# Whole gathered rows of V for the second 128 tokens, and one pass over V for the first 128

## Chip, cores and metric

The kernel runs on 1 core of one Trainium2 chip. The metric is the device time of one execution in microseconds (us); the profile is one execution taken by the hardware profiler.

## The reference, cut to what matters

The program is two transformer blocks over 256 tokens of width 1024, in float32. Only the last layer of the second block, a product-key expert layer, is touched by the change:

```python
def block(xb):                       # xb: 128 tokens x 1024; called for 2 blocks of tokens
    ...                              # query, top 16 of 2 x 128 keys, top 16 of 16 x 16, in 8 heads
    idx = ...                        # 128 tokens x 8 heads x 16 experts, out of 16384 experts
    gate = jax.nn.softmax(best_s, axis=-1)
    h = jax.nn.gelu(jnp.einsum('thkd,td->thk', u_table[idx], xb), approximate=False)
    return jnp.einsum('thk,thkd->td', gate * h, v_table[idx])
```

u_table and v_table are 16384 rows of 1024 floats each (64 MB per table). Each token picks 128 rows (slots) of both. The layer's result is added to x (times ALPHA) and a layer norm ends the kernel.

## The kernel before, in words

**Tokens and slots.** Tokens stand on the 128 partitions, in two blocks t = 0 and t = 1. `gather(dst, tab, idx, s)` (line 1377) is an indirect DMA from POOL's queue that fetches, for slot s, one table row for each of the 128 tokens: 512 KB for whole rows, 256 KB for half rows.

**U.** For each slot, `u_dot` (line 1404) gathers a row of U for each token and lets DVE multiply it with x and sum it (line 1408). For some slots `u_mm` (line 1380) has PE transpose the gathered rows (1392), ACT copy them (1393) and PE multiply them with x (1396); `u_diag` (1399) has DVE pick the diagonal. `weights` (1420) turns the sums into coefficients by a Gelu on ACT and a product on DVE.

**V as a dense product.** `AT[t]` is a matrix of coefficients, 128 tokens x 16384 experts, made from one-hot rows by `spread_low` (ACT, 1425) and `spread` (DVE, PE, ACT, 1432), 32 groups each for a token block. With it, a sum over chosen rows becomes a product with all of V: 128 blocks of 128 rows, in PE matmuls with 512 columns, two instructions for each.

**The order of the last stages.** DVE's order is that of the program text (`manual_schedule`); the other engines' order is fixed when the kernel is built. Gathers stand one behind the other on POOL's queue, and loads of V on SP's.

1. The loop of lines 1509 to 1525 handles U for t = 0.
2. The loop of lines 1592 to 1627 handles U for t = 1, slot n by slot n: 18 slots with n below 36 by `u_mm`, 110 by `u_dot`. In steps 0 to 35 it also spreads AT[0] (32 groups, LOW = 36); in steps 0 to 63 (SEL = 64) it advances the selection (`later`) of the last three pairs of heads of t = 1 by 47 items in 18 steps and 94 items in 46 steps; from step 38 `hdense` multiplies AT[0] with the upper 512 columns of V (line 1581), whose 64 loads of 512 KB (two row blocks of half rows each, line 1569) go through 4 to 6 buffers. At n = 64 two constants of the last norm are loaded on POOL's queue (line 94), into memory that the selection used. The gathered rows of U have 6 buffers in pool `ub`, and 8 more in pool `sec` up to step 64.
3. Lines 1643 to 1674: the coefficients of t = 1, then the second half of the making of AT[1] (`high1`).
4. Lines 1719 to 1737: the lower 512 columns of V are loaded (line 1636, 64 loads of 512 KB) and multiplied with AT[0] and AT[1] (line 1641). The upper 512 columns for t = 1 are fetched as gathered half rows (`v_load`, 128 gathers of 256 KB) and added by DVE (`v_add`, line 1466). The layer norm of t = 0 (`end`) runs beside the last steps, that of t = 1 at the end.

Of the kernel before, what the change touches and what calls it, by code (L numbers as in the profile page):

```python
# [23 lines left out]
def block_kernel(ctx: ExitStack, tc: tile.TileContext, I, out):  # L24
    nc = tc.nc
# [1117 lines left out]
    vhalf = vtab.rearrange("e (a d) -> (e a) d", a=2)  # L1143
    io = pe_.tile([128, 128], F, name="io")
    G.iota(io, pattern=[[1, 128]], base=0, channel_multiplier=0, allow_small_or_imprecise_dtypes=True)
    idx_u, idx_v, ex_all, gate_all, hd_all, sc_all, c_all, tr_all = ({} for _ in range(8))
    for t in range(2):
        idx_u[t] = pe_.tile([128, 128], I32, name=f"idxu{t}")
        idx_v[t] = pe_.tile([128, 128], I32, name=f"idxv{t}")
# [178 lines left out]
    def select(t, h0, nh, early=False):  # L1328
# [33 lines left out]
        V.tensor_scalar(idx_v[t][:, hs], idx_u[t][:, hs], 2.0, 1.0, op0=OP.mult, op1=OP.add)  # L1362
# [5 lines left out]
    def u_tile(t, s):  # L1368

        if t and second and s % 7 >= 3:  # L1370
            return second[0].tile([128, D], F, tag="u", name="ust", bufs=8)
        if t == 0 and s % 3 == 2:
            return ux.tile([128, D], F, tag="u", name="ust")
        return ub.tile([128, D], R, tag="u", name="u").bitcast(F)
# [5 lines left out]
    def u_mm(t, s):  # L1380
# [51 lines left out]
    def spread(t, q):  # L1432
# [4 lines left out]
        both = q % (3 if t == 0 else 2) == 0  # L1437
# [99 lines left out]

    secx = ExitStack()
    sec = secx.enter_context(tc.tile_pool(name="sec", bufs=1, side="right"))
    xF1 = sec.tile([128, 8, 128], F, name="xF1")  # L1540
    for c in range(2):
        A.activation(out=xF1[:, 4 * c:4 * c + 4], in_=half_T(x2[:, 1], c), func=AF.Copy)
    second += [sec, xF1]
# [12 lines left out]
    hs_, hb = {}, iter(range(64))  # L1556

    def hload():
        b = next(hb, None)
        if b is None:  # L1560
            return
        if late_h:
            w = ub.tile([128, D], R, tag="u", name="wh").bitcast(F)
        elif second and b % 6 >= 4:
            w = sec.tile([128, D], F, tag="h", name="wh", bufs=2)
        else:
            w = h_tile("wh")
        hs_[b] = w.rearrange("p (b c) -> p b c", b=2)
        nc.sync.dma_start(out=hs_[b], in_=vtab[b * 256:(b + 1) * 256, 512:].rearrange("(b p) c -> p b c", p=128))

    hn = iter(range(64))

    def hdense():
        b = next(hn, None)
        if b is None:
            return False
        hload()
        w = hs_.pop(b)
        for i in range(2):
            n = b * 2 + i  # L1580
            T.matmul(acc2, lhsT=AT[0][:, :, n], rhs=w[:, i], start=n == 0, stop=n == 127)  # L1581
        return True

    late_h = []
    s2 = chain(*(select(1, h, 2) for h in (2, 4, 6)))
    SEL, LOW, HN = 64, 36, 38

    H1 = 58
    MMS1 = range(1, LOW, 2)

    later = chain(paced(s2, TWO, 18), paced(s2, 2 * TWO, SEL - 18))
    for n in range(128):
        assert (1, n // 16) in ready
        if n in MMS1:
            due[n + 5] = (u_mm(1, n), 1, n)
        else:
# [9 lines left out]
        if n == LOW - 10:  # L1606
            for _ in range(6):
                hload()
        if n >= HN:
            m, k = 128 - HN, n - HN  # L1610
            for _ in range(k * H1 // m, (k + 1) * H1 // m):
                hdense()
        if n == SEL:
# [15 lines left out]
    late_h.append(1)
    acc = [pa(), pa()]  # L1630
    wt = {}

    def vload(b):
        w = ub.tile([128, D], R, tag="u", name="w").bitcast(F)
        wt[b] = w.rearrange("p (b c) -> p b c", b=2)
        nc.sync.dma_start(out=wt[b], in_=vtab[b * 256:(b + 1) * 256, 0:512].rearrange("(b p) c -> p b c", p=128))

    def dense(t, b):
        for i in range(2):
            n = b * 2 + i  # L1640
            T.matmul(acc[t], lhsT=AT[t][:, :, n], rhs=wt[b][:, i], start=n == 0, stop=n == 127)  # L1641

    weights(1, 0, 128)
# [5 lines left out]
    left = [128]

    def v_next():
        s = next(vq, None)
        if s is not None:
            ahead.append((s, v_load(s)))
        if not ahead:
            return False
        s, v = ahead.pop(0)
        v_add(s, v)
        left[0] -= 1
        if not left[0]:  # L1660
            V.bn_stats(out=st[:, 1, 1], in_=x2[:, 1, 512:])
        return True

    PRE = 6
    for q in high1:
        spread(1, q)
        if q % 2 == 0:
            hdense()
        if q >= 4:
            v_next()  # L1670
    while hdense():
        v_next()
    for b in range(PRE):
        vload(b)
    V.scalar_tensor_tensor(x2[:, 0, 512:], x2[:, 0, 512:], ALPHA, acc2, op0=OP.mult, op1=OP.add)
    V.bn_stats(out=st[:, 0, 1], in_=x2[:, 0, 512:])
    o2 = out[0].rearrange("(t p) d -> t p d", p=128)

    def low_half(t):
        z = x2[:, t, :512]  # L1680
        if t == 0:
            V.scalar_tensor_tensor(z, z, ALPHA, acc[t], op0=OP.mult, op1=OP.add)
        else:
            V.tensor_tensor(z, z, acc[t], op=OP.add)
        yield
        V.bn_stats(out=st[:, t, 0], in_=z)
# [83 lines left out]
```

## Time and profile before

| | |
|---|---|
| median of 3 runs | 1452.6 us (1452.05 to 1454.0) |
| the profiled execution | 1450.03 us, of which the span of its instructions is 1448.3 us |
| busy share of the span | PE 89%, PE weight loads 73%, DVE 67%, ACT 41%, POOL 31% |
| bytes moved by DMA | 338.58 MB, 234 GB/s over the span |
| mean granted TensorE clock | 0.975 of full speed |

The shares are means over stages with different limits, so the last 560 us have to be read by stages. Of the two DMA queues that matter, q0 carries what POOL issues (gathers) and q1 what SP issues (loads of weights and of V).

### The profile page before, as it was taken

The numbers are of one execution on the slowest core, as the hardware profiler recorded it, in microseconds if no ns is written. First come the engines' busy times: TensorE is split into PE (matmuls) and PEld (weight loads), VectorE is DVE, ScalarE is ACT, GpSimd is POOL, SyncE is SP. The second block draws the span as 40 slices with busy tenths as digits, with TensorE's granted clock in tenths as the row PEclk, the third lists the DMA queues.
The fourth block names the chain that finished last, engine by engine and source line by source line (L and its number), as shares of the span: only waits on it lengthen the run. The fifth ranks groups of instructions, "written<-read, shape, count | busy, mean of one in ns | idle before, by whom it ended". The sixth has DMA issues, their size and how long they took to land.

```text
span 1448.3 us, 20024 instructions
## 1 busy us (share of the span) xinstructions
PE 1290.2 (89%) x7068; PEld 1056.9 (73%) x7068; DVE 974.5 (67%) x2345; ACT 590.0 (41%) x1194; POOL 451.0 (31%) x420
## 2 busy tenths in 40 slices
PE   8999999998999999998998955997765697999996
PEld 7988998976897778987888855894432366666664
DVE  5687655577575486587899987989766549555303
ACT  6465544464455731232232398770292036000000
POOL 2000000001000000003678876544454236777301
PEclk9999999999999999998999977999999999999999
DMA  7435555555454330065999999879999976999741
GB/s 235 146 117 181 188 189 186 188 166 161 141 160 136 113 101 1 7 196 203 361 346 370 330 364 349 271 234 357 404 407 408 375 258 170 368 331 348 259 158 69
DMA packets 132821, 338.58 MB, mean 234 GB/s; under 512 B 11675, under 2 KB 15089, under 8 KB 132721
## 3 DMA queue, kind: packets, MB, share of 16 engines
q1 hardware_dynamic: 83680, 165.01, 34.7%
q0 software_dynamic: 48288, 170.98, 32.3%
q10 hardware_dynamic: 752, 1.31, 0.3%
q8 instruction: 56, 0.92, 0.3%
q14 instruction: 45, 0.36, 0.1%
HBM read 336.21 MB, written 1.05 MB: 233 GB/s over the span
## 4 chain that ended last, share of the span: by engine, by line
PE 69%; DMA 13%; ACT 9%; DVE 7%; issue 1%; SPq 0%; DVEq 0%; ACTq 0%
PE pa L1641 15%; DMA wh<-in_peer_v_dram 10%; PE pa L217 8%; PE pa L219 8%; PE pa L218 8%; PE pa L1396 4%; PE pb L1448 3%; PE pa L1581 3%; ACT AT L1429 3%; PE pb L217 2%; PE pb L219 2%; PE pb L218 2%; PE pa L1187 2%; PE pb L963 2%; DMA AT<-in_peer_w_q_dram 2%; ACT uT L1393 1%
## 5 line engine op out<-in xcount | busy, mean ns | idle before, releaser
L212 DVE TENSOR_TENSOR w<-raw,w 128x1024 fp32r<-128x1024 f32 (+2 forms) x162 | 197.7, 1224 | 117.9 <-ACT w L211 117.4
L211 ACT ACTIVATE w<-raw 128x1024 fp32r<-128x1024 f32 (+2 forms) x164 | 172.9, 1061 | 168.8 <-PE pa L219 68.9
L1377 POOL DMA_INDIRECT u<-in_peer_u_dram,idxu x178 | 198.2, 1113 | 126.6 <-DVE jk L1408 60.0
L1408 DVE SCALAR_TENSOR_TENSOR jk<-u,xa 128x1024 bf16<-128x1024 f32 x159 | 193.7, 1218 | 51.3 <-DMA u<-in_peer_u_dram,idxu 50.7
L1641 PE MATMUL pa<-w,AT 128*128 128x512 f32 x512 | 222.7, 595 | 1.0 <-ACT AT L1449 0.7
L1641 PEld LDWEIGHTS pa<-w,AT 128*128 128x128 f32 x512 | 150.4, 296 | 68.8 <-DMA w<-in_peer_v_dram 2.1
L1581 PE MATMUL pa<-wh,AT 128*128 128x512 f32 x256 | 128.5, 639 | 63.1 <-DMA wh<-in_peer_v_dram 62.4
L1377 POOL DMA_INDIRECT v<-in_peer_v_dram,idxv x128 | 134.6, 1052 | 78.1 <-issue 25.4
L1581 PEld LDWEIGHTS pa<-wh,AT 128*128 128x128 f32 x256 | 72.3, 298 | 118.5 <-DMA wh<-in_peer_v_dram 94.7
L1396 PE MATMUL pa<-xF,uT 128*128 128x128 f32 x800 | 112.6, 298 | 28.3 <-ACT uT L1393 26.7
L1466 DVE SCALAR_TENSOR_TENSOR xa<-v,c,xa 128x512 f32<-128x512 f32 x128 | 96.0, 750 | 59.6 <-DMA v<-in_peer_v_dram,idxv 58.0
L1396 PEld LDWEIGHTS pa<-xF,uT 128*128 128x128 f32 x800 | 102.6, 207 | 38.7 <-ACT uT L1393 38.3
L1377 POOL DMA_INDIRECT ust<-in_peer_u_dram,idxu x78 | 94.8, 1215 | 61.6 <-PE pb L1392 29.3
L94 POOL DMA_DIRECT2D ln_g<-in_ln_g_dram x2 | 1.1, 572 | 291.0 <-PE pb L1105 285.0
L1702 ACT ACTIVATE xa<-xa,nmu 128x512 f32<-128x512 f32 x3 | 2.1, 716 | 206.6 <-DVE nmu L1696 206.6
L1429 ACT ACTIVATE AT<-io,tr 128x128 f32<-128x128 f32 x256 | 82.4, 402 | 0.4 <-DVE jk L1408 0.3
L1448 PE MATMUL pb<-e,AT 128*128 128x128 f32 x512 | 68.9, 280 | 11.6 <-ACT e L1447 11.5
L217 PE MATMUL pb<-xt,w 128*128 128x256 f32 (+2 forms) x272 | 77.0, 283 | 0.0
L218 PE MATMUL pb<-xt,w 128*128 128x256 f32 (+2 forms) x272 | 76.7, 282 | 0.0
L219 PE MATMUL pb<-xt,w 128*128 128x256 f32 (+2 forms) x272 | 76.6, 281 | 0.0
L1448 PEld LDWEIGHTS pb<-e,AT 128*128 128x128 f32 x512 | 63.0, 191 | 17.2 <-ACT e L1447 14.1
L217 PE MATMUL pa<-w,xt 128*128 128x512 f32 x176 | 71.6, 412 | 1.4 <-ACT w L211 1.0
(534 smaller groups left out, 2752.8 us busy)
## 6 DMA issues: line engine op xcount, KB each, us to landing
raw<-in_mlp_w_dram SPq DMA_DIRECT2D x64, 512.0 KB, 3.6
wh<-in_peer_v_dram SPq DMA_DIRECT2D x64, 512.0 KB, 12.7
w<-in_peer_v_dram SPq DMA_DIRECT2D x64, 512.0 KB, 6.7
raw<-in_w_in_dram SPq DMA_DIRECT2D x38, 512.0 KB, 3.5
raw<-in_mlstm_w_in_dram SPq DMA_DIRECT2D x20, 512.0 KB, 3.6
AT<-in_peer_w_q_dram SPq DMA_DIRECT2D x12, 512.0 KB, 19.1
raw<-in_mlstm_w_out_dram SPq DMA_DIRECT2D x8, 512.0 KB, 3.8
raw<-in_ple_gate_w_dram SPq DMA_DIRECT2D x8, 512.0 KB, 3.8
```

What stands on the lines that cost most here:

```text
L211: A.activation(out=w1[:, :kn * cn], in_=raw[:, :kn * cn], func=AF.Copy)
L212: (eng or V).tensor_tensor(w2[:, :kn * cn], raw[:, :kn * cn], w1[:, :kn * cn].bitcast(F), op=OP.subtract)
L217: T.matmul(o, lhsT=a1, rhs=b1, start=start, stop=False)
L218: T.matmul(o, lhsT=a1, rhs=b2, start=False, stop=False)
L219: T.matmul(o, lhsT=a2, rhs=b1, start=False, stop=stop)
L1377: G.indirect_dma_start(out=dst, out_offset=None, in_=tab, in_offset=bass.IndirectOffsetOnAxis(ap=idx[:, s:s + 1], axis=0))
L1396: T.matmul(o[:, :128], lhsT=uT[:, k], rhs=xT[:, k], start=k == 0, stop=k == 7)
L1408: V.scalar_tensor_tensor(jk, u, 1.0, x2[:, t], op0=OP.mult, op1=OP.mult, accum_out=hd_all[t][:, s:s + 1])
L1429: A.activation(out=g[:, n], in_=io, func=AF.Square, bias=tr_all[t][:, 1, q * 4 + n:q * 4 + n + 1])
L1448: T.matmul(ps[:, i * 128:(i + 1) * 128], lhsT=g[:, i], rhs=e1[:, i], start=True, stop=True)
L1581: T.matmul(acc2, lhsT=AT[0][:, :, n], rhs=w[:, i], start=n == 0, stop=n == 127)
L1641: T.matmul(acc[t], lhsT=AT[t][:, :, n], rhs=wt[b][:, i], start=n == 0, stop=n == 127)
```

## The change

For t = 1, V is no longer multiplied with a coefficient matrix: all 1024 columns of each chosen row are gathered (128 gathers of 512 KB) and added by DVE. AT[1], its making, the second index table `idx_v` and the product of t = 1 with the lower half of V go. For t = 0, V is loaded once in whole rows (128 loads of 512 KB) and each block is multiplied in two halves, into two PSUM tiles. The gathered rows of t = 1, first of U and then of V, share one ring of 13 buffers (`ring1`); the loads of V use the 6 buffers of `ub` and the 4 of `wraw`, 9 loads ahead. All 128 slots of t = 1 go by `u_dot`. AT[0] is spread in 24 steps instead of 36. `blocks_at` spreads the 128 blocks evenly over steps 24 to 243 of the two loops (128 slots of U, then 128 of V).

```diff
-        if t and second and s % 7 >= 3:
-            return second[0].tile([128, D], F, tag="u", name="ust", bufs=8)
+        if t:
+            return ring1[0].tile([128, D], F, tag="u", name="u1", bufs=13)
...
     def v_load(s):
-        if not vts:
-            w = h_tile("v")
-            vts[1], v = w[:, 512:], w[:, :512]
-        else:
-            v = vts.pop(1)
-        gather(v, vhalf, idx_v[1], s)
+        v = u_tile(1, s)
+        gather(v, vtab, idx_u[1], s)
         return v
...
-        z = x2[:, 1, 512:]
-        V.scalar_tensor_tensor(z, v, c_, z, op0=OP.mult, op1=OP.add)
+        z = x2[:, 1]
+        V.scalar_tensor_tensor(z, v, c_all[1][:, s:s + 1], z, op0=OP.mult, op1=OP.add)
...
+    ring1.append(ctx.enter_context(tc.tile_pool(name="ring1", bufs=1, side="right")))
...
+    def vload():
+        n = next(to_load, None)
+        if n is not None:
+            held[n] = h_tile("w") if n % 5 in (1, 3) else ub.tile([128, D], R, tag="u", name="w").bitcast(F)
+            nc.sync.dma_start(out=held[n], in_=vtab[n * 128:(n + 1) * 128, :])
+
+    def dense():
...
+        vload()
+        w = held.pop(n)
+        for c in range(2):
+            T.matmul(acc[c], lhsT=AT[0][:, :, n], rhs=w[:, c * 512:c * 512 + 512], start=n == 0, stop=n == 127)
...
-    SEL, LOW, HN = 64, 36, 38
+    SEL, LOW, AHEAD = 64, 24, 9
...
+    LAST = 244
+
+    def blocks_at(n):
+        for _ in range((n - LOW) * 128 // (LAST - LOW), (n + 1 - LOW) * 128 // (LAST - LOW)):
+            dense()
+
     for n in range(128):
         assert (1, n // 16) in ready
-        if n in MMS1:
-            due[n + 5] = (u_mm(1, n), 1, n)
-        else:
-            u_dot(1, n)
-        if n in due:
-            u_diag(*due.pop(n))
+        u_dot(1, n)
...
+        if n == 8:
+            for _ in range(AHEAD):
+                vload()
+        if n >= LOW:
+            blocks_at(n)
         if n == SEL:
...
-            at1 = ctx.enter_context(tc.tile_pool(name="at1", bufs=1, side="right"))
-            AT.append(at1.tile([128, 128, 128], F, name="AT1"))
-            for i in range(2):
-                slots_T(1, ex_all[1][:, i], i)
...
+        if n == 100:
+            weights(1, 0, 64)
...
     A.activation(out=x2[:, 1], in_=x2[:, 1], func=AF.Copy, scale=ALPHA)
...
+    END = 118
+    end = chain(half_sum(0), half_sum(1), last_norm(0))
+    ahead = [v_load(s) for s in range(12)]
+    for s in range(128):
+        if s < 116:
+            ahead.append(v_load(s + 12))
+        v_add(s, ahead.pop(0))
+        if s == 8:
+            weights(1, 64, 128)
+        blocks_at(128 + s)
+        if s >= END:
+            advance(end)
```

## Rows read from the trace of the kernel before

**Rows 1.** Page, part 4: the chain that ended last, by engine and line.
```profile
PE 69%; DMA 13%; ACT 9%; DVE 7%; issue 1%; SPq 0%; DVEq 0%; ACTq 0%
PE pa L1641 15%; DMA wh<-in_peer_v_dram 10%; PE pa L217 8%; PE pa L219 8%; PE pa L218 8%; PE pa L1396 4%; PE pb L1448 3%; PE pa L1581 3%; ACT AT L1429 3%; PE pb L217 2%; PE pb L219 2%; PE pb L218 2%; PE pa L1187 2%; PE pb L963 2%; DMA AT<-in_peer_w_q_dram 2%; ACT uT L1393 1%
```

**Rows 2.** The same chain in order of time: start us, us, engine and line.
```profile
991.63 17.41 DMA wh<-in_peer_v_dram
...
1166.95 10.68 DMA w<-in_peer_v_dram
...
1227.41 209.82 PE pa L1641 x488
```

**Rows 3.** Stretches: length; PE, PEld, DVE, ACT, POOL busy us (instructions); PE clock, DMA share, GB/s.
```profile
740.00:780.00 40.00, 37.19 (x311) 34.71 (x310) 38.11 (x128) 12.99 (x28) 32.27 (x26) 1.00 0.95 344
780.00:820.00 40.00, 35.27 (x283) 33.04 (x282) 37.61 (x120) 9.18 (x22) 32.46 (x25) 0.96 0.98 366
...
850.00:880.00 30.00, 15.94 (x89) 14.98 (x88) 26.25 (x56) 30.00 (x89) 23.14 (x21) 0.73 0.96 352
...
940.00:960.00 20.00, 19.21 (x165) 18.40 (x165) 16.66 (x60) 14.42 (x36) 9.78 (x10) 1.00 0.75 240
...
1000.00:1020.00 20.00, 12.22 (x26) 7.18 (x26) 19.96 (x55) 0.69 (x4) 8.31 (x7) 1.00 1.04 404
...
1120.00:1140.00 20.00, 10.45 (x20) 5.50 (x20) 12.46 (x21) 0.00 (x0) 9.82 (x11) 1.00 1.04 409
...
1230.00:1270.00 40.00, 40.00 (x94) 27.52 (x94) 22.18 (x31) 0.00 (x0) 31.08 (x30) 1.00 0.98 357
```

**Rows 4.** DMA queues from 1040 to 1100 us: packets, MB, share of 16 engines.
```profile
q0 software_dynamic: 4369, 15.93, 66.4%
q1 hardware_dynamic: 4366, 8.42, 36.9%
```

**Rows 5.** Timeline of DVE: slots 0, 36, 63 and 64 of t = 1.
```profile
892.10 1.22 DVE L1408 SCALAR_TENSOR_TENSOR jk<-u,xa 128x1024 bf16<-128x1024 f32 x1
...
975.98 1.22 DVE L1408 SCALAR_TENSOR_TENSOR jk<-u,xa 128x1024 bf16<-128x1024 f32 x1
...
1024.99 1.22 DVE L1408 SCALAR_TENSOR_TENSOR jk<-u,xa 128x1024 bf16<-128x1024 f32 x1
...
1026.25 1.22 DVE L1408 SCALAR_TENSOR_TENSOR jk<-u,xa 128x1024 bf16<-128x1024 f32 x1
```

**Rows 6.** Groups on DVE, 892 to 977 us: busy us, mean ns, idle before.
```profile
L1439 DVE TENSOR_TENSOR e<-tr,io 128x512 f32<-128x512 f32 x21 | 14.3, 679 | 5.4 <-PE pb L1448 5.4
L1445 DVE TENSOR_SCALAR e<-io,tr 128x128 f32<-128x128 f32 x44 | 12.2, 354 | 2.8 <-PE pb L1448 2.8
...
L1401 DVE SCALAR_TENSOR_TENSOR jk<-pa,ident 128x128 bf16<-128x128 f32 x15 | 4.4, 291 | 0.5
```

**Rows 7.** Timeline of POOL between the two U loops: start us, us, [idle before].
```profile
877.94 0.96 POOL L1377 DMA_INDIRECT u<-in_peer_u_dram,idxu  x1 [0.30 <-issue]
879.21 0.96 POOL L1377 DMA_INDIRECT u<-in_peer_u_dram,idxu  x1 [0.30 <-issue]
...
886.28 1.13 POOL L1377 DMA_INDIRECT ust<-in_peer_u_dram,idxu  x1 [4.85 <-DVE jk L1408]
```

**Rows 8.** Who DVE waited for, 1036 to 1153 us: us, times, longest.
```profile
DVE jk L1408 <- DMA u<-in_peer_u_dram,idxu: 47.5, 59, 3.6
```

**Rows 9.** Tile v: DVE's adds in the timeline, and issue to landing of its gathers.
```profile
1347.93 3.11 DVE L1466 SCALAR_TENSOR_TENSOR xa<-v,c,xa 128x512 f32<-128x512 f32 x4 [1.89 <-DMA v<-in_peer_v_dram,idxv]
...
DMA to landing us min/median/max: 3.3/6.1/7.6
```

**Rows 10.** Timeline of POOL at step 64: the constants of the last norm.
```profile
1025.62 0.57 POOL L94 DMA_DIRECT2D ln_g<-in_ln_g_dram  x1 [5.98 <-issue]
```

**Rows 11.** Timeline of the end: DVE's last norm, t = 1.
```profile
1437.97 0.69 DVE L1686 BATCH_NORM_STATS2 st<-xa 128x6 f32<-128x512 f32 x1
1438.70 0.21 DVE L1692 BATCH_NORM_AGGREGATE bnag<-st 128x2 f32<-128x12 f32 x1
```

More of the change, by code (lines that the diff above doesn't have):

```diff
@@ L1535, in h_tile @@
         return wraw.tile([128, WF], F, tag="raw", name=name)[:, :D]
[L1538 to L1543, printed above, removed]
+    ring1.append(ctx.enter_context(tc.tile_pool(name="ring1", bufs=1, side="right")))
     weights(0, 0, 128)
     slots_T(0, c_all[0], 2)
-    acc2 = pa()
-    low1, high1 = iter(range(32)), iter(range(32))
-    SP = 2
+    acc = [pa(), pa()]
     def spread_next(f, it, t, *a):
@@ L1554, in spread_next @@
             f(t, q, *a)
[L1556 to L1560, printed above, removed]
-            return
[L1562 to L1578, printed above, removed]
-        for i in range(2):
[L1580 to L1584, printed above, removed]
+    held, to_load, to_add = {}, iter(range(128)), iter(range(128))
+    def vload():
[4 more added lines that the diff above has]
+    def dense():
+        n = next(to_add, None)
+        if n is None:
+            return
+        vload()
+        w = held.pop(n)
+        for c in range(2):
+            T.matmul(acc[c], lhsT=AT[0][:, :, n], rhs=w[:, c * 512:c * 512 + 512], start=n == 0, stop=n == 127)
     s2 = chain(*(select(1, h, 2) for h in (2, 4, 6)))
-    SEL, LOW, HN = 64, 36, 38
-    H1 = 58
-    MMS1 = range(1, LOW, 2)
+    SEL, LOW, AHEAD = 64, 24, 9
     later = chain(paced(s2, TWO, 18), paced(s2, 2 * TWO, SEL - 18))
+    LAST = 244
+    def blocks_at(n):
+        for _ in range((n - LOW) * 128 // (LAST - LOW), (n + 1 - LOW) * 128 // (LAST - LOW)):
+            dense()
     for n in range(128):
         assert (1, n // 16) in ready
-        if n in MMS1:
-            due[n + 5] = (u_mm(1, n), 1, n)
-        else:
-            u_dot(1, n)
-        if n in due:
-            u_diag(*due.pop(n))
+        u_dot(1, n)
         if n < SEL:
@@ L1629, in block_kernel @@
[L1629 to L1643, printed above, removed]
+        if n == 100:
+            weights(1, 0, 64)
@@ L1644, in block_kernel @@
+    assert next(low0, None) is None and not due
     A.activation(out=x2[:, 1], in_=x2[:, 1], func=AF.Copy, scale=ALPHA)
-    vq = iter(range(128))
-    ahead = [(s, v_load(s)) for s in [next(vq) for _ in range(6)]]
-    slots_T(1, c_all[1], 2)
     st = pe_.tile([128, 2, 2, 6], F, name="st")
[L1649 to L1676, printed above, removed]
-    o2 = out[0].rearrange("(t p) d -> t p d", p=128)
[L1679 to L1684, printed above, removed]
+    o2 = out[0].rearrange("(t p) d -> t p d", p=128)
@@ L1685, in low_half, with half_sum @@
+    def half_sum(c):
+        z = x2[:, 0, c * 512:c * 512 + 512]
+        V.scalar_tensor_tensor(z, z, ALPHA, acc[c], op0=OP.mult, op1=OP.add)
         yield
-        V.bn_stats(out=st[:, t, 0], in_=z)
+        V.bn_stats(out=st[:, 0, c], in_=z)
         yield
@@ L1714, in last_norm @@
             nc.sync.dma_start(out=o2[t][:, cs], in_=z[:, cs])
-    end = chain(low_half(0), last_norm(0))
-    END = 10
-    VN = left[0]
-    for b in range(0, 64, 2):
-        for i in (b, b + 1):
-            if i >= PRE:
-                vload(i)
-        for t in range(2):
-            if t == 0 or b < 58:
-                dense(t, b)
-                dense(t, b + 1)
-        if b < 62:
-            for _ in range((b // 2 + 1) * VN // 31 - b // 2 * VN // 31):
-                v_next()
-    for b in range(58, 64):
-        dense(1, b)
-    while v_next():
-        if left[0] < END:
+    END = 118
[9 more added lines that the diff above has]
+        if s >= END:
             advance(end)
+    assert next(to_add, None) is None
     advance(end, 1000)
-    for _ in chain(low_half(1), last_norm(1)):
+    for c in range(2):
+        V.bn_stats(out=st[:, 1, c], in_=x2[:, 1, c * 512:c * 512 + 512])
+    for _ in last_norm(1):
         pass
```

31 lines of the change are left out of this document (5 added, 26 removed).

## The prediction

> **What bounds the kernel now.** I read the chain that ended last first, then the stretches of the span, then single waits. The chain is 69% PE and 13% DMA over the whole span [rows 1], but in order of time the two take turns: from 991 to 1167 us it is waits for loads of V with short matmuls between them, and from 1227 to 1437 us it is PE without a gap, 488 instructions in 209.8 us, so 0.43 us each [rows 2]. The stretches say the same from the other side [rows 3]. From 1000 to 1140 us DMA carries 404 to 409 GB/s, and DVE waits there for gathered rows of U, 47.5 us in all [rows 8]: that loop is bound by DMA. From 940 to 960 us DMA carries 240 GB/s and DVE and PE are busy: bound by compute. From 1230 us PE is busy throughout, DMA below its best. So the last 556 us, from slot 0 of t = 1 at 892.1 us [rows 5] to the end at 1448.3, have three limits, and the change trades PE time in the third for DMA bytes in all of them.
>
> **Bytes.** I count in buffers of 512 KB (524,288 bytes): at 406 GB/s, the middle of the two rows of [rows 3], one takes 1.29 us. Before: 128 gathers of U, 128 half gathers of V (64 buffers), 128 loads of V: 320 buffers, 413 us of DMA in the 556 us. After: 128 + 128 gathers and 128 loads: 384 buffers, 496 us. The change costs 64 buffers, 83 us of DMA time; it takes away half of the 512 instructions of line 1641 (256 x 0.43 = 110 us of PE) and the second half of the making of AT[1], the 60 us between 1166.95 and 1227.41 us on the chain [rows 2]. If DMA could run at 406 GB/s from 892 us on, the end would be near 892 + 496 + 16 (the tail, below) = 1404 us. What follows is how far it falls short.
>
> **Steps 0 to 23, bound by DVE.** Before, steps 0 to 35 took 892.10 to 975.98 us [rows 5]: 18 dots at 1.27 us (slots 63 and 64 start 1.26 apart, [rows 5]; the same spacing stands all along), 15 diagonals at about 0.37 with their 0.08 read-out, the spreading of AT[0] at 14.3 + 12.2 us and 8.2 us of waits for PE [rows 6], and selection. Up to slot 63 it is 132.9 us; less 45 dots (57.2), 18 diagonals (6.7), spreading and its waits (34.7) leaves 34 us for 141 items of selection, 0.24 each. After: the whole spreading stays, 24 dots stand where 18 stood (+7.6), the 15 diagonals go (-5.6), 12 steps of selection come later (24 items, -6). Step 24 begins near 975.98 - 4 = 972 us. I leave the waits for PE as they are, though PE loses the transposes of `u_mm`; without them it is 964. The start could also slip: gathers went out into buffers of `ub` up to some us before 886.28, the first into `sec` at 886.28, when DVE released memory [rows 7]. After, all of t = 1 wait for that memory. A gather lands in 6.1 us [rows 9], so slot 0 is there at 892 to 893: no delay, at worst 4 us with nine loads of V beside it. By 972 us DMA has fetched 24 + 13 gathers and 10 loads: 47 buffers, 61 us of its time. Of the 86 us since 886 it idles about 25, since the rings are full and no block of V can be used before AT[0] is spread. That is the largest loss.
>
> **From step 24 to the last load of V, bound by DMA.** DVE needs until 1026.25 + 18 x (1.27 - 0.37) = 1042 us for step 64. From 972 PE multiplies as loads come: a block is four instructions, 4 x 0.43 = 1.72 us, a third more than the 1.29 us of its load, but DMA shares its time. How it shares is to be seen in [rows 4]: q0 with rows of 4 KB and q1 with rows of 2 KB moved 4369 and 4366 packets, one for one, hence bytes two for one. With whole rows on both, I take one load for one gather, 2.58 us a pair; PE is then busy 67% of the time. 70 us to 1042 hold 54 buffers: 64 gathers landed, 37 loads. DVE's pace is just met. The remaining 91 loads go with 91 gathers: 182 x 1.29 = 235 us, to 1277.
>
> Two waits lie in this part. At step 64 the constants of the last norm wait on POOL's queue for the selection to end (5.98 us of idle before, [rows 10]); behind them stand gathers which the ring of 13 would have let go up to 13 steps earlier. DMA meanwhile has loads of V, at PE's pace of 1.72 us: 25 us at 0.75 of its rate, 6 us at most; I take 2. Where the loops meet, slots of V reuse the ring's buffers as dots release them, so gathers go on; DVE waits about 1 us for the scaling of x. The 10 index products of `idx_v` (0.18 us each), the diagonals after step 24, PE's transposes and ACT's copies cost nothing either way: DVE, PE and ACT all have idle time there once DMA is the limit, as DVE has 7.5 of 20 us from 1120 us [rows 3].
>
> **The gathers left.** 64 + 91 = 155 of 256 have landed at 1277; 101 remain, now alone. DMA would take 101 x 1.29 = 130 us. POOL can issue one in 0.96 + 0.30 = 1.26 us [rows 7], but its means are longer: busy plus 0.30 each gives 1.40 us (850 to 880 us), 1.54 (740 to 780) and 1.60 (780 to 820), and in these three stretches, with gathers alone, DMA carried 352, 344 and 366 GB/s [rows 3]. Twelve are already issued, so 89 x 1.40 + 6.1 = 131 us; with 1.26 it is 118 (DMA's 130 decides), with 1.60 149. DVE's add of 512 columns takes 0.78 us in a row of four [rows 9], the dot of 1024 columns 1.27; an add of 1024 lies between 1.17 (a dot without its read-out) and 1.56; as the same form of instruction it should be near the dot, 1.25, 126 us. I take 131 us, for POOL is as loaded here as at 850 to 880 us: to 1408.
>
> **Tail.** The norm of t = 0 comes between the last ten adds: about 4 us of DVE. Then the last add (1.25), two statistics (1.4), and from the aggregate to the end as before, 1448.3 - 1438.7 = 9.6 [rows 11]: 16 us. The end is at 1277 + 2 + 131 + 16 = 1426 us. The profiled execution lasted 1.7 us longer than its span and 2.6 us less than the median: **1430 us** by the median, 1.6% less than 1452.6.
>
> **Rival 1: whole rows on both queues don't reach 406 GB/s.** For: with gathers alone DMA carried only 344 to 366 GB/s at a share of 0.95 to 0.98, and 357 at 0.98 in the mixture from 1230 us [rows 3]. Against: in the second POOL, in the third PE was full, so neither shows DMA's limit, while 404 to 409 held for 140 us with DVE waiting. After 972 us 337 buffers (176.7 MB) are left; at 352 GB/s they take 502 us, the end is 972 + 502 + 18 = 1492, by the median 1496: slower by 3%. It decides from 386 GB/s: below that, 458 us are not enough. Chance 0.13. The Trainium skill, DMA: Bandwidth & Descriptors, Specifications, gives about 358 GB/s as a core's share of HBM; by that alone the estimate would be 494 us for these bytes, 8 us less than this rival's. [rows 3] show 404 to 409 on this core, so the measurement decides against it as a ceiling here.
>
> **Rival 2: the last gathers are bound by POOL or DVE.** At 1.60 us the end is 18 us later, 1448 by the median: same or barely faster. If a gather could be issued only between two adds, 1.25 + 0.95 = 2.2 us, 89 take 196 + 6 = 202 us, and it is 1501. It turns slower (25.5 us later) from 1.69 us per gather. Against: from 850 to 880 us, with DVE busy 26.25 of 30 us, POOL still issued 21 gathers, one in 1.43 us [rows 3]. Chance 0.10, a third of it slower. The Trainium skill, SBUF — State Buffer, section SBUF: two separate sides, has such a lock between VectorE and GpSimd, which for two SBUF inputs it limits to GpSimd instructions that read SBUF; the row from 850 us shows no such stop.
>
> **Rival 3: the compressed spreading holds.** If PE and ACT can't follow in 24 steps, or the first loads of V push back the first gathers, AT[0] is ready later. Each us later costs about 0.7 us, since only 47 of 66 buffers' time is used until then. 20 us late gives 1444; 32 no gain. Chance 0.07.
>
> **Rival 4: less is lost.** AT[0] ready at 964 (-6), DMA at 409 GB/s (-3), no stop at step 64 (-2), the norm of t = 0 hidden (-4): 1415. Chance 0.10.
>
> **Chances and range.** The forecast holds 0.60, its own range 1418 to 1446. A measurement of this kernel can tell about 0.2% from no change, 1449.7 to 1455.5. Faster: forecast, rival 4, and parts of 2 and 3, 0.76; same 0.07, between the cases; slower 0.17: rival 1 and the far ends of 2 and 3. For 8 in 10 the range reaches from 1403 (all DMA time used, 1404 + 4, less a little) to 1458; above lies most of rival 1.
>
> **What would show it.** Right: no L1448 after about 975 us; step 24 near 972; q0 and q1 with equal packets and bytes from there, 400 GB/s or more; loads of V done near 1277, long before their steps of the text; then gathers alone, POOL 1.3 to 1.5 us each; chain DMA instead of PE in the last 400 us. Wrong: DMA below 386 GB/s while both queues are full; DVE or POOL without idle time and DMA with some in the last 130 us; AT[0] ready after 990 us; the queues not sharing one for one, which by itself moves the end little.

## The result, and the profile after

The changed kernel takes 1435.57 us (median of 4 runs, 1434.49 to 1436.67) where the kernel before took 1453.3 us (4 runs): ratio 0.9877, interval 0.9859 to 0.9894, so 1.2% faster. 1430 us was forecast. The profiled execution lasted 1436.67 us with a span of 1434.9 us, against the 1426 us of the prediction's sum. The rest asks where these 9 us went, whether the mechanisms were the ones named, and what holds the kernel up now.

The chain that ended last, by engine and line, answers to [rows 1]:

```profile
PE 50%; DMA 20%; DVE 18%; ACT 6%; issue 5%; POOL 0%; SPq 0%; DVEq 0%; POOLq 0%; ACTq 0%
DMA u<-in_peer_u_dram,idxu 11%; DVE xa L1454 9%; PE pa L217 8%; PE pa L219 8%; PE pa L218 8%; DMA u<-in_peer_v_dram,idxu 5%; PE pa L1185 3%; PE pb L1442 3%; PE pb L217 2%; PE pb L219 2%; PE pb L218 2%; PE pa L1390 2%; DVE jk L1402 2%; ACT AT L1423 2%; PE pb L963 2%
```

The 15% of the product with the lower half of V are gone from it. What stands in their place is gathers (11% and 5%) and DVE's adds (9%, line 1454). The adds were not foreseen on the chain.

Stretches of the changed kernel, to be read beside [rows 3]: length; PE, PEld, DVE, ACT, POOL busy us (instructions); PE clock, DMA share, GB/s:

```profile
930.00:950.00 20.00, 13.39 (x65) 12.07 (x64) 18.49 (x49) 13.09 (x35) 5.88 (x6) 0.67 0.51 157
950.00:970.00 20.00, 14.72 (x69) 13.66 (x70) 18.04 (x54) 11.82 (x32) 6.35 (x7) 0.67 0.59 175
970.00:990.00 20.00, 17.95 (x55) 12.97 (x54) 19.41 (x56) 4.80 (x15) 9.74 (x11) 0.99 0.84 302
1000.00:1020.00 20.00, 18.36 (x40) 10.91 (x38) 20.00 (x65) 0.00 (x0) 11.73 (x9) 1.00 1.03 411
1120.00:1140.00 20.00, 16.33 (x33) 8.83 (x32) 9.54 (x17) 0.00 (x0) 11.02 (x8) 1.00 1.03 413
...
1330.00:1370.00 40.00, 0.00 (x0) 0.00 (x0) 38.92 (x31) 0.00 (x0) 30.86 (x31) 0.50 1.02 402
...
889.80:975.40 85.60, 54.28 (x257) 48.84 (x257) 75.41 (x216) 50.49 (x132) 40.82 (x39) 0.67 0.72 245
975.40:1285.70 310.30, 259.76 (x511) 142.66 (x512) 181.78 (x339) 4.13 (x12) 167.26 (x127) 1.00 1.02 409
```

Three parts, with three limits. From the first gather of t = 1 to the first product (the seventh row) DVE is busy 88% and DMA carries 245 GB/s. From the first product to the last, DMA carries 409 GB/s on average and 411 to 413 once it is going, with every engine below its full time after 1120 us. After that DVE is busy 38.92 of 40 us and DMA is at 402.

The ends of the middle part, from the products' line (shortest, median, longest ns; first and last start), and the two queues from 1100 to 1200 us (packets, MB, share of 16 engines), which answer to [rows 4]:

```profile
L1550 PE MATMUL pa<-w,AT x512: 592/592/804, 975.4 to 1285.7; 128*128 128x512 f32 x171
```

```profile
q0 software_dynamic: 5648, 20.57, 51.3%
q1 hardware_dynamic: 5649, 20.58, 51.2%
```

POOL at the start of t = 1 and at step 64, which answer to [rows 7] and [rows 10]:

```profile
889.80 1.14 POOL L1374 DMA_INDIRECT u<-in_peer_u_dram,idxu  x1 [9.48 <-issue]
...
1061.17 0.54 POOL L94 DMA_DIRECT2D ln_b<-in_ln_b_dram  x1 [1.63 <-DMA u<-in_peer_u_dram,idxu]
1064.14 1.42 POOL L1374 DMA_INDIRECT u<-in_peer_u_dram,idxu  x1 [2.43 <-DMA u<-in_peer_u_dram,idxu]
```

The first gather into the ring goes out at 889.80 us, where 886.28 was counted on; the stop at step 64 is 2.43 us.

DVE where the last products are done, and at the end, which answer to [rows 9] and [rows 11]:

```profile
1282.98 1.28 DVE L1454 SCALAR_TENSOR_TENSOR xa<-u,c,xa 128x1024 f32<-128x1024 f32 x1 [1.26 <-DMA u<-in_peer_v_dram,idxu]
1284.91 15.81 DVE L1454 SCALAR_TENSOR_TENSOR xa<-u,c,xa 128x1024 f32<-128x1024 f32 x12 [0.64 <-DMA u<-in_peer_v_dram,idxu]
...
1421.22 1.28 DVE L1454 SCALAR_TENSOR_TENSOR xa<-u,c,xa 128x1024 f32<-128x1024 f32 x1
...
1422.74 1.28 DVE L1639 BATCH_NORM_STATS2 st<-xa 128x6 f32<-128x512 f32 x2
1424.06 0.21 DVE L1600 BATCH_NORM_AGGREGATE bnag<-st 128x2 f32<-128x12 f32 x1
```

Up to 1283 us each add waits 1.26 us for its row: a gather lands every 2.5 us, since a load of V goes between. From 1284.91 us on twelve adds stand in 15.81 us without a wait, 1.32 us each. At that moment the limit passes from DMA to DVE: from then to the last add DVE waits for no row. POOL is as full there, with one gather in 1.02 + 0.30 = 1.32 us:

```profile
1322.99 1.02 POOL L1374 DMA_INDIRECT u<-in_peer_v_dram,idxu  x1 [0.30 <-issue]
1324.31 1.02 POOL L1374 DMA_INDIRECT u<-in_peer_v_dram,idxu  x1 [0.30 <-issue]
```

So both are at their limit, at the same pace; the third experiment takes work from DVE.

### The profile page after: what moved, and what is told of

The parts are those of the page before. It is cut to its first block, busy times and chain, and to the rows that moved or that the text cites. A ratio compares the mean times of both kernels' runs of the same rounds, so it can differ in the third digit from the quotient of the medians.

```text
span 1434.9 us, 17753 instructions
## 1 busy us (share of the span) xinstructions
PE 1139.5 (79%) x6113; PEld 916.3 (64%) x6113; DVE 1030.9 (72%) x2255; ACT 478.7 (33%) x898; POOL 484.1 (34%) x420
## 4 chain that ended last, share of the span: by engine, by line
PE 50%; DMA 20%; DVE 18%; ACT 6%; issue 5%; POOL 0%; SPq 0%; DVEq 0%; POOLq 0%; ACTq 0%
DMA u<-in_peer_u_dram,idxu 11%; DVE xa L1454 9%; PE pa L217 8%; PE pa L219 8%; PE pa L218 8%; DMA u<-in_peer_v_dram,idxu 5%; PE pa L1185 3%; PE pb L1442 3%; PE pb L217 2%; PE pb L219 2%; PE pb L218 2%; PE pa L1390 2%; DVE jk L1402 2%; ACT AT L1423 2%; PE pb L963 2%
## 5 line engine op out<-in xcount | busy, mean ns | idle before, releaser
L1374 POOL DMA_INDIRECT u<-in_peer_u_dram,idxu x214 | 261.1, 1220 | 194.9 <-DMA u<-in_peer_u_dram,idxu 71.9
L1402 DVE SCALAR_TENSOR_TENSOR jk<-u,xa 128x1024 bf16<-128x1024 f32 x203 | 247.1, 1217 | 96.2 <-DMA u<-in_peer_u_dram,idxu 95.7
L1550 PE MATMUL pa<-w,AT 128*128 128x512 f32 x512 | 260.4, 637 | 51.2 <-DMA w<-in_peer_v_dram 50.5
L1454 DVE SCALAR_TENSOR_TENSOR xa<-u,c,xa 128x1024 f32<-128x1024 f32 x128 | 165.5, 1293 | 37.8 <-DMA u<-in_peer_v_dram,idxu 33.2
L1374 POOL DMA_INDIRECT u<-in_peer_v_dram,idxu x128 | 145.9, 1140 | 69.7 <-DMA u<-in_peer_v_dram,idxu 36.0
L1390 PE MATMUL pa<-xF,uT 128*128 128x128 f32 x512 | 75.4, 308 | 25.9 <-ACT uT L1387 24.7
L1390 PEld LDWEIGHTS pa<-xF,uT 128*128 128x128 f32 x512 | 69.0, 217 | 33.0 <-ACT uT L1387 33.0
L1442 PE MATMUL pb<-e,AT 128*128 128x128 f32 x256 | 53.8, 385 | 25.7 <-ACT e L1441 23.5
L217 PE MATMUL pa<-w,xt 128*128 128x512 f32 x176 | 71.1, 408 | 1.3 <-ACT w L211 1.0
L219 PE MATMUL pa<-w,xt 128*128 128x512 f32 x176 | 70.7, 402 | 0.0
L218 PE MATMUL pa<-w,xt 128*128 128x512 f32 x176 | 70.3, 400 | 0.0
L1442 PEld LDWEIGHTS pb<-e,AT 128*128 128x128 f32 x256 | 48.7, 278 | 31.0 <-ACT e L1441 28.2
L217 PE MATMUL pa<-xt,w 128*128 128x256 f32 x240 | 68.3, 284 | 0.0
L219 PE MATMUL pa<-xt,w 128*128 128x256 f32 x240 | 68.1, 284 | 0.0
## 6 DMA issues: line engine op xcount, KB each, us to landing
w<-in_peer_v_dram SPq DMA_DIRECT2D x128, 512.0 KB, 20.3
raw<-in_mlp_w_dram SPq DMA_DIRECT2D x64, 512.0 KB, 3.9
raw<-in_w_in_dram SPq DMA_DIRECT2D x38, 512.0 KB, 3.6
raw<-in_mlstm_w_in_dram SPq DMA_DIRECT2D x20, 512.0 KB, 3.7
AT<-in_peer_w_q_dram SPq DMA_DIRECT2D x12, 512.0 KB, 17.4
raw<-in_mlstm_w_out_dram SPq DMA_DIRECT2D x8, 512.0 KB, 3.4
raw<-in_ple_gate_w_dram SPq DMA_DIRECT2D x8, 512.0 KB, 3.4
raw<-in_w_o_dram SPq DMA_DIRECT2D x8, 512.0 KB, 4.8
```

The lines of the kernel that those rows point to most:

```text
L217: T.matmul(o, lhsT=a1, rhs=b1, start=start, stop=False)
L218: T.matmul(o, lhsT=a1, rhs=b2, start=False, stop=False)
L219: T.matmul(o, lhsT=a2, rhs=b1, start=False, stop=stop)
L1374: G.indirect_dma_start(out=dst, out_offset=None, in_=tab, in_offset=bass.IndirectOffsetOnAxis(ap=idx[:, s:s + 1], axis=0))
L1390: T.matmul(o[:, :128], lhsT=uT[:, k], rhs=xT[:, k], start=k == 0, stop=k == 7)
L1402: V.scalar_tensor_tensor(jk, u, 1.0, x2[:, t], op0=OP.mult, op1=OP.mult, accum_out=hd_all[t][:, s:s + 1])
```

## The experiments

The theory after this reading (D): from the first product to the end the time is set by bytes, at one load for one gather, PE being covered; before it, DMA stands still in part, and that is the largest loss. Its rivals: the middle is bound by PE, which is busy 84% of it; the last part is bound by DVE or POOL; what costs is the spreading of AT[0] being late, or being squeezed into 24 steps, rather than DMA standing still.

On the chip of runs 5 to 8 the kernel before itself took 1543 us, so their ratios can't stand beside the others; those four are compared with one another and by stretches inside their traces.

**1. Half the bytes of V's loads.** The upper half of the first tokens' product is left out.

```diff
-            nc.sync.dma_start(out=held[n], in_=vtab[n * 128:(n + 1) * 128, :])
+            nc.sync.dma_start(out=held[n][:, :512], in_=vtab[n * 128:(n + 1) * 128, :512])
...
-            T.matmul(acc[c], lhsT=AT[0][:, :, n], rhs=w[:, c * 512:c * 512 + 512], start=n == 0, stop=n == 127)
+            T.matmul(acc[c], lhsT=AT[0][:, :, n], rhs=w[:, :512], start=n == 0, stop=n == 127)
```

> Each load of V fetches only 512 columns (256 KB) and both matmuls use them, so 64 of the 384 buffers of 512 KB are not moved; the upper half of the product for the first 128 tokens is left out. Theory A (DMA at 412 GB/s sets the pace from the first product to the last load): packets are still shared one for one, a pair is 0.75 buffer, 1.91 us instead of 2.56; the loads end near 1199 us instead of 1285, and the end comes 80 to 90 us earlier, near 1350 us. Theory B (PE sets the pace, its work is unchanged): 1436 us. Theory C (DVE's dots and adds set the pace throughout): 1436 us.

Measured: 1360.34 us (before: 1454.22), ratio 0.9353 (0.9334 to 0.9372); 75 us less than the changed kernel, with as many matmuls. A stretch of it, and its queues from 1100 to 1190 us:

```profile
1000.00:1200.00 200.00, 199.93 (x430) 120.83 (x429) 144.09 (x251) 3.44 (x8) 145.33 (x105) 1.00 1.03 404
```

```profile
q0 software_dynamic: 6650, 24.21, 67.8%
q1 hardware_dynamic: 6646, 12.11, 35.5%
```

The bytes decide, not PE: 64 buffers less are worth 82 us at 1.28 us each, and 75 came (80 to 90 were expected). DMA holds 404 GB/s with whole rows on one queue and half rows on the other, still packet for packet. PE is now full too, so here the two limits meet, which may be what the rest of the gain went into; 404 is only a lower bound for what DMA can do.

**2. PE's work doubled.** Each block is multiplied a second time into PSUM tiles that nobody reads.

```diff
+            T.matmul(spare[c], lhsT=AT[0][:, :, n], rhs=w[:, c * 512:c * 512 + 512], start=n == 0, stop=n == 127)
```

> Each block of V is multiplied twice, the second time into two PSUM tiles that nobody reads: 512 more PE instructions of 0.43 us, 220 us of PE. Theory A (DMA): the stream of V slows to PE's 3.44 us a block, the gathers take the DMA time that it leaves, both end near 1410 us; 1430 to 1442 us in all, no change or a little less. Theory B (PE sets the pace): some 200 us more, 1640 us.

Measured: 1443.43 us, ratio 0.9924 (0.9908 to 0.9941). Two stretches:

```profile
1000.00:1280.00 280.00, 280.00 (x654) 192.75 (x653) 191.88 (x305) 3.44 (x8) 193.10 (x140) 1.00 1.03 411
1280.00:1400.00 120.00, 120.00 (x281) 82.42 (x281) 78.41 (x62) 0.00 (x0) 84.14 (x63) 1.00 1.03 411
```

Twice the products cost 8 us, a little more than expected. PE takes 438 us for them (976.9 to 1415.3) and slows the loads, but the gathers take the DMA time that the loads leave: 411 GB/s throughout. The 8 us come at the end, where DVE, in the norm of t = 0, waits 8.85 us for the last products, with the last adds behind it:

```profile
1414.24 0.69 DVE L1593 SCALAR_TENSOR_TENSOR xa<-xa,pa 128x512 f32<-128x512 f32 x1 [8.85 <-PE pa L1550]
```

So PE as such has slack, and the products may be spread over the gathers that are left.

**3. Half of each add.** The upper 512 columns of the second tokens' sum are left out.

```diff
-        z = x2[:, 1]
-        V.scalar_tensor_tensor(z, v, c_all[1][:, s:s + 1], z, op0=OP.mult, op1=OP.add)
+        z = x2[:, 1, :512]
+        V.scalar_tensor_tensor(z, v[:, :512], c_all[1][:, s:s + 1], z, op0=OP.mult, op1=OP.add)
```

> The adds of gathered rows of V take only 512 of 1024 columns on DVE (0.78 instead of 1.32 us); half of that sum is left out. Theory D (in the last 125 us, with gathers alone, DVE's adds at 1.32 us set the pace and its backlog ends last): the gathers go at DMA's 1.27 us, the backlog goes, 1422 to 1428 us. Theory E (POOL's issue at 1.32 us, or DMA, sets that stretch): 1434 to 1436 us.

Measured: 1429.76 us, ratio 0.9831 (0.9814 to 0.9847), 6 us less. In the last part:

```profile
1330.00:1370.00 40.00, 0.00 (x0) 0.00 (x0) 22.99 (x31) 0.00 (x0) 30.40 (x32) 0.50 1.03 409
...
L1454 DVE SCALAR_TENSOR_TENSOR xa<-u,c,xa x128: 750/752/1545, 1217.2 to 1415.2; 128x512 f32<-128x512 f32 x128
```

DVE's adds were the limit of the last part, by little: with adds of 0.75 instead of 1.285 us DVE has idle time, DMA carries 409 instead of 402 GB/s, and 6 us are gained. The next limit lies just behind: gathers alone run at 404 to 410 GB/s in this kernel. From 1327 to 1362 us POOL issued one every 1.25 us, faster than the 1.28 us that DMA took for one, so its issuing isn't that limit, though it lies close too.

**4. The spreading in 36 steps again.**

```diff
-    SEL, LOW, AHEAD = 64, 24, 9
+    SEL, LOW, AHEAD = 64, 36, 9
```

> AT[0] is spread over 36 steps again, instead of 24; all else as in the changed kernel. Theory A by bytes: the first product starts near 995 instead of 975 us, but 12 more gathers are done by then; 21 us less 12 x 1.27: 5 to 7 us more, 1441 us. By the price in the prediction's third rival (0.7 us for each us): 14 us more, 1450 us. If the start of the products does not matter: 1436 us.

Measured: 1435.82 us, ratio 0.9883 (0.9867 to 0.99): no change. From the first gather to the first product:

```profile
885.99:986.80 100.81, 60.13 (x258) 53.01 (x258) 95.45 (x273) 51.86 (x136) 53.37 (x51) 0.60 0.79 269
```

The first product comes at 986.8 instead of 975.4 us, and the end is where it was. AT[0] may be 15 us later after the first gather at no cost, if DVE spends these 15 us on twelve more dots: their gathers (12 x 1.28 us of DMA) needn't be made later.

**5 to 8, on the other chip.** In the fifth, ten slots of U go by PE and ACT again (`u_mm`), with a ring of 10 for want of memory; the sixth has the ring of 10 alone; in the seventh, 14 of the last 54 rows of V are added on PE, by a diagonal matrix that ACT makes, and all blocks of V are multiplied by step 200; the eighth spreads in 12 steps.

```diff
+    MMS1 = range(1, LOW - 4, 2)
...
-        u_dot(1, n)
+        if n in MMS1:
+            due[n + 5] = (u_mm(1, n), 1, n)
+        else:
+            u_dot(1, n)
+        if n in due:
+            u_diag(*due.pop(n))
```

> Ten slots of U of the second tokens (1, 3, ... 19) go by PE and ACT again instead of by a dot on DVE; their buffers are taken from the ring, which has 10 instead of 13. Theory A (DVE's work sets when AT[0] is ready): 10 x 0.9 us less on DVE, so the first product near 966 instead of 975 us, but 3 fewer gathers are fetched ahead (3.8 us): 1430 us. Theory F (the spreading waits for PE and ACT, whose work grows by 10 x 3 us and 10 x 1.2 us): first product at 980 us or later, 1440 us or more.

```diff
-            return ring1[0].tile([128, D], F, tag="u", name="u1", bufs=13)
+            return ring1[0].tile([128, D], F, tag="u", name="u1", bufs=10)
```

> The ring of gathered rows has 10 buffers instead of 13, all else unchanged. Theory A (by bytes: while AT[0] is spread DMA stands still with full rings, so each buffer fewer is 1.27 us of DMA time later): 4 us more, 1439 us. If the ring's depth does not matter: 1435 to 1436 us. If gathers starve with 10: well over 1440 us.

```diff
+    def v_mm(s, v):
+        dg = gt_.tile([128, 4, 128], F, tag="e1", name="dg")[:, 0]
+        A.activation(out=dg, in_=ident, func=AF.Copy, scale=c_all[1][:, s:s + 1])
+        for c in range(2):
+            T.matmul(acc1[c], lhsT=dg, rhs=v[:, c * 512:c * 512 + 512], start=s == PES[0], stop=s == PES[-1])
...
-        v_add(s, ahead.pop(0))
+        (v_mm if s in PES else v_add)(s, ahead.pop(0))
```

> 14 of the last 54 rows of V (slots 74, 78, ... 126) are added on PE, as a product with a diagonal of the coefficients that ACT makes, into two PSUM tiles that DVE adds at the end; the blocks of V stand earlier in the program's order. Theory D (DVE's adds set the last stretch): 14 x 1.32 us less and 1.4 more on DVE; then DMA sets it: 5 to 8 us less, 1428 to 1431 us. Theory E (POOL or DMA already set it): 1436 us or more.

```diff
-    SEL, LOW, AHEAD = 64, 24, 9
+    SEL, LOW, AHEAD = 64, 12, 9
```

> AT[0] is spread over 12 steps instead of 24. By bytes: 12 fewer gathers are done when the first product starts (15 us of DMA), which can start at most 15 to 22 us earlier if PE and ACT follow: 1430 to 1436 us. If PE and ACT set the spreading already in 24 steps (DVE waited 5 us for PE there), the start comes only a few us earlier: 1440 to 1450 us.

Measured: 1457.08, 1454.71, 1456.26 and 1460.36 us. Taking dots from DVE gains nothing (the fifth beside the sixth, which has the same ring). The seventh gains nothing that shows either, but the changed kernel with its ring of 13 was not run on this chip, so there is nothing to set its time against. Spreading in 12 steps is the slowest of the four. Stretches and a POOL instruction of the seventh with adds on PE, and the first part of the eighth:

```profile
1370.00:1410.00 40.00, 21.31 (x28) 7.11 (x28) 26.60 (x22) 2.81 (x7) 25.96 (x28) 0.70 0.91 355
...
1370.00:1396.00 26.00, 15.05 (x19) 5.02 (x20) 19.74 (x16) 1.21 (x3) 19.60 (x22) 0.68 1.02 407
...
1402.95 0.94 POOL L1374 DMA_INDIRECT u<-in_peer_v_dram,idxu  x1 [6.12 <-remote]
```

```profile
899.10:982.20 83.10, 51.03 (x257) 46.57 (x257) 55.05 (x157) 49.73 (x131) 25.94 (x27) 0.71 0.52 180
```

In the seventh DVE has idle time from then on, and up to 1396 us DMA carries 407 GB/s, against 402 in the changed kernel with DVE at its limit. Then ACT, which makes the diagonals, stands still for 9.4 us and POOL for 6.12, and the stretch to 1410 us comes to 355 GB/s. What held them the trace doesn't name. So what speaks against the relief in this run is the stop, and not DMA's rate before it. In the eighth DVE is busy 66% and DMA half of its time: with 12 steps the spreading is limited by what lies between DVE, PE and ACT (DVE waits 15.2 us for PE's L1442, against 5.5 in the changed kernel), and too few gathers are asked for.

**9. The changed kernel again**, beside runs 10 and 11.

> The changed kernel once more, unaltered, as the measure for the two runs beside it on the same chip: 1434 to 1437 us where the kernel before takes 1453.

Measured: 1433.65 us (before: 1453.39), ratio 0.9867 (0.9848 to 0.9886), as in the result.

**10. Both at once: 36 steps and 16 slots by `u_mm`**, with the ring of 10. The edit is that of the fifth, with LOW = 36.

> AT[0] is spread over 36 steps and 16 slots of U (1, 3, ... 31) go by PE and ACT instead of DVE, as in the kernel before; the ring has 10 buffers. By bytes: 36 instead of 24 steps take about the same 88 us to the first product, since DVE has 16 dots less; 12 more gathers are done by then (15.3 us of DMA), 3 fewer are ahead (3.8): 8 to 12 us less than the changed kernel beside it. If PE and ACT set the spreading: no gain or a loss.

Measured: 1437.76 us, ratio 0.9889 (0.9871 to 0.9907): no gain, where 8 to 12 us were expected by bytes.

**11. The same, with 19 rows of V added on PE** among the blocks (slots 34 to 124, every fifth; all blocks done by step 160).

```diff
+    PES = range(34, 127, 5)
...
-    LAST = 244
+    LAST = 160
```

> As the run before, and 19 rows of V (slots 34, 39, ... 124) are added on PE instead of DVE, so that DVE's 1.32 us an add no longer sets the stretch with gathers alone: another 3 to 6 us less by DMA's 1.27 us a gather. If PE's adds hold the ring's buffers too long: no gain.

Measured: 1445.54 us, ratio 0.9939 (0.9919 to 0.996), 8 us more than the tenth. A stretch of its last part:

```profile
1330.00:1370.00 40.00, 17.56 (x20) 5.37 (x18) 24.40 (x19) 2.01 (x5) 32.78 (x24) 0.59 0.89 312
```

24 gathers in 40 us, 1.37 us busy each instead of 1.0 in the changed kernel: 24 x (1.37 + 0.30) = 40, so POOL issues without a pause and is the limit, at 312 GB/s. Why its instruction is longer here was not found.

**12. No spreading.** The product takes the one-hot rows as they are, so the first tokens' sum is left without its coefficients.

```diff
-            spread(0, order0[q])
```

> The changed kernel with the spreading of the first 24 steps' coefficients over the product's rows (the matmuls L1442 and the VectorE operations behind them) left out altogether; the product takes the selection rows as they are, so the first 128 tokens' sum lacks its coefficients. The spreading of the later steps, done among the gathers, stays. It prices all that the wait for the first 24 steps costs. By the prediction's step on steps 0 to 23 (the transfers idle 25 to 29 us before the first product because every buffer is full), the first product comes near 905 us instead of 975, the transfers are saturated from there, the 128 paired loads end by 1215 to 1218, the gathers that are left follow at 1.32 us each, and the time is 1405 to 1410. By the pattern of the two runs with 36 and 12 steps (what the start gains, the gathers landed before it lose) the gain is smaller: about 41 us or more of earlier start less the gathers not yet landed, 1410 to 1425. If the late start costs nothing: 1434 to 1436.

Measured: 1401.3 us (1400.24 to 1403.57; before: 1455.89), ratio 0.9639 (0.9605 to 0.9673): 32 to 34 us less than the changed kernel, more than either theory had put down from the prediction's 25 to 29 us of idle DMA. The first product and a stretch:

```profile
L1550 PE MATMUL pa<-w,AT x512: 592/592/1223, 887.9 to 1201.9; 128*128 128x512 f32 x171
```

```profile
900.00:1200.00 300.00, 249.07 (x488) 135.10 (x486) 181.43 (x413) 3.61 (x14) 159.07 (x118) 1.00 1.03 411
```

The edit takes away DVE's 26.5 us of spreading together with the wait for AT[0], so it prices the two as one. From 900 us DMA has no idle time, and the span, 1398.5 us, is under the 1404 us that the prediction worked out for DMA at 406 GB/s from 892 us on.

**What the twelve say together.** This was worked out after the runs. In each trace, take the stretch from the first gather of t = 1 to the first product, and count the DMA time in it that 409 GB/s would have left unused: for the changed kernel 85.6 x (1 - 245 / 409) = 34.3 us. Its end is 1434.9 - 889.8 = 545.1 us after the first gather, so 510.8 us plus the unused time. The same difference for the others that move the same bytes:

| run | first gather | first product | GB/s between | unused, us | end | end - first gather - unused |
|---|---|---|---|---|---|---|
| changed kernel | 889.8 | 975.4 | 245 | 34.3 | 1434.9 | 510.8 |
| 9, again | 886.9 | 971.9 | 246 | 33.9 | 1431.2 | 510.4 |
| 4, 36 steps | 886.0 | 986.8 | 269 | 34.5 | 1431.4 | 510.9 |
| 10, 36 steps and `u_mm` | 890.2 | 990.0 | 257 | 37.1 | 1439.0 | 511.7 |
| 5, `u_mm` | 906.6 | 992.2 | 227 | 38.1 | 1455.4 | 510.7 |
| 6, ring of 10 | 898.8 | 987.8 | 217 | 41.8 | 1450.9 | 510.3 |
| 7, adds on PE | 900.7 | 992.0 | 230 | 40.0 | 1453.9 | 513.2 |
| 8, 12 steps | 899.1 | 982.2 | 180 | 46.5 | 1458.4 | 512.8 |
| 12, no spreading | 885.1 | 887.9 | 208 | 1.4 | 1398.5 | 512.0 |

The last column moves by 3 us while the first product moves by 104. The bytes are the same in all nine, so the column has to stand still as long as DMA is full from the first product on; that it does is what the table shows. Neither when AT[0] is ready nor in how many steps matters by itself: each us in which DMA has nothing to fetch before the first product costs one us, and a later start costs what it is late. Where the bytes, the last part's limit or PE's end change, the last column does too: 438.3 us in the first run, 503.4 in the third (half adds), 517.1 in the second (the late norm), 524.6 in the eleventh (POOL's limit).

## Why the prediction was right, and where its terms were off

**The trade of PE time for bytes: as described.** The length from the first gather to the first product was put at 972 - 886.28 = 85.7 us; it is 85.6. From the last product to the end 131 + 16 = 147 were counted; it is 149.2. The 9 us are: 3.5 for the first gather (889.8), 3.3 in the middle (310.3 us against 305 + 2) and 2.2 at the end (149.2 against 147).

**The start (+3.5).** The prediction allowed 4 us of delay and took none. In the eight other traces from chips where the kernel before takes 1453 to 1456 us, the first gather of t = 1 goes out anywhere from 885.1 to 890.3 us, so this is within what one execution differs from another.

**Steps 0 to 23, bound by DVE: right.** Groups on DVE from 890 to 976 us, which answer to [rows 6]:

```profile
L1433 DVE TENSOR_TENSOR e<-tr,io 128x512 f32<-128x512 f32 x21 | 14.3, 683 | 4.8 <-PE pb L1442 4.7
L1439 DVE TENSOR_SCALAR e<-io,tr 128x128 f32<-128x128 f32 x44 | 12.2, 357 | 0.8 <-PE pb L1442 0.8
```

The spreading costs DVE the same 14.3 and 12.2 us, with 5.6 us of waits for PE instead of 8.2. The choice to keep these waits in the sum was the safe one.

**"It idles about 25": the step that was mis-sized.** It was called the largest loss, which the twelfth run bears out, but it is 34 us: of the ten loads counted into this time, most had landed before the first gather went out (q1 moves only 1.34 MB after it), so that 21 MB, 40 buffers, moved after it and not 47 (245 GB/s x 85.6 us). The end doesn't move by this, since by the first product about 37 gathers and 10 loads had landed, as in the sum.

**One load for one gather, 2.58 us a pair: right.** 5648 and 5649 packets, 20.57 and 20.58 MB; an add every 2.56 us. The Trainium skill, DMA: Bandwidth & Descriptors, section Queues, rings and completion order, says that each DMA engine takes turns between the queues at packet granularity; this trace and that of the first run (6650 and 6646 packets with 24.21 and 12.11 MB) agree. What the profile counts as a packet is about one row here (20.57 MB / 5648 = 3.6 KB), so the traces show equal turns, not how much a turn holds. At 1284.91 us 101 adds were left, as counted. The middle is 3.3 us longer than the sum because more went through it: 126.88 MB, 242 buffers, where the sum has 54 + 182 = 236. Two of the six are the constants of the last norm, 512 KB each, of which the sum counted the wait and not the bytes (a DMA list of the trace has `ln_g` and `ln_b` with 512.0 KB each); the others are gathers. Six at 1.28 us are 7.7; the 2 us for step 64 that weren't needed and 409 instead of 406 GB/s give 4.3 of it back.

**The stop at step 64: there, and harmless.** POOL stood 2.43 us, as [rows 10] suggested, but gathers and loads already queued kept DMA at 411 GB/s from 1000 us on.

**The gathers left: the sum right, the engine wrong.** The step took 1.40 us for POOL's issuing of each gather, giving 131 us, and 1.25 us for an add. An add takes 1.285 us and comes every 1.32, and 101 x 1.32 = 133 us; POOL's instruction takes only 1.02 us while adds run back to back, one gather in 1.32 us as well. With half adds (third run) POOL issues one in 0.94 to 0.98 + 0.30 us, DVE waits for rows and the stretch is shorter; a faster POOL alone could not have helped, since DVE had no idle time. So the stretch is bound by DVE, 4 to 6 us above DMA's own time. That 131 and 133 lie so close is luck: one is POOL's price for 89 gathers, the other DVE's for 101 adds. Rival 2 was near the truth in kind, far from it in size: a turn to slower needed 1.69 us per gather.

**Rival 1 (whole rows don't reach 406 GB/s): out.** 409 GB/s over 310 us, 411 to 413 inside it; the deciding rate was 386. Gathers alone, too, reach 402 GB/s here, so the 344 to 366 in [rows 3] were not DMA's limit; that POOL and PE held them there, as the prediction argued, no run shows.

**Rival 3: its price was wrong.** "Each us later costs about 0.7 us" held for no run. In the fourth the first product is 15 us later after the first gather at no cost; in the twelfth, without spreading, the gain is the unused DMA time. Dots without a wait come every 1.28 us on DVE (1201.51 and 1202.79 us in the twelfth run), and a gather takes 1.28 us of DMA: as long as DVE does dots while it delays AT[0], one pays for the other. Squeezing 36 steps into 24 was thus worth nothing, and 12 steps are worse.

**Rival 4: half of it came.** DMA ran at 409 GB/s and the stop at step 64 cost nothing, but AT[0] was ready at 975 us and not at 964, and the norm of t = 0 cost the 4 us that were counted: the last nine adds, with it between them, take 16.1 us instead of 11.9.

**Not settled.** A deeper ring should let DMA work on during the spreading; memory is full, and it wasn't tried. The ring of 10 in the sixth run left 41.8 us unused where the seventh, with 13 on the same chip, left 40.0. Of the 34 us that the spreading costs, moving dots to PE and ACT recovers none. No version that computes everything beat the changed kernel.

## What to carry to other kernels

When a stage trades engine time for bytes, first make the sum of all bytes still to move at the rate that the trace shows while DMA is full, then look for every stretch in which DMA will have nothing to fetch: here the end, less the start and less the time in which DMA had nothing to fetch, is the same in nine traces within 3 us. Work may be moved between steps at no gain when the engine that does it and the transfers it releases take equal times (1.28 us each); here only work taken out of the way of the transfers altogether (the twelfth run) counted. Before relieving an engine that looks full, ask what is next and how far behind: DVE was full in the last part, and halving its adds gave 6 us, since DMA and POOL were within 0.1 us a gather of being full too.

## What the runs showed of the hardware that was not expected

- The same kind of gather instruction keeps POOL busy for different times: 1.37 to 1.42 us on average among the loads of V, 1.02 while DVE adds back to back, 0.94 to 0.98 when these adds are halved, 1.37 on average in the last part of the eleventh run. What makes it vary was not found.
- The granted TensorE clock is 0.67 of full speed on average from 930 to 970 us, a mixture of its levels of 2.4 and 1.2 GHz, with PE busy 67 to 74%; before, with `u_mm` beside the spreading, PE was busy 96% at 1.00 [rows 3]. Yet DVE waited less for PE than before.
- The sixteen DMA engines carried 411 GB/s for 300 us without a break, from two queues with 4 KB rows, one of them gathered. The Trainium skill, DMA: Bandwidth & Descriptors, Specifications, puts a core's share of HBM at about 358 GB/s; with one core at work these traces show more.
- On one chip the kernel before took 1543 us instead of 1453, while the changed kernel's relatives took some 20 us more than elsewhere: their first gather of t = 1 came 9 to 21 us later, and more DMA time was unused before the first product; after it the rate was the same. The kernel before had a mean granted clock of 0.94 to 0.95 there instead of 0.97 to 0.98. No profile of the kernel before was taken there, so the cause is open.
